# First block of a two-block transformer: weight splits off GpSimd, rotated halves kept in place, scores as 32-row products of four heads, the first expert quad interleaved

## The chip, the cores and the metric

The kernel runs on one core of one Trainium2 chip. The metric is the device time of one execution in microseconds, as the median of the runs shown. The engines of the core are named as in the profile: PE (TensorE, matmuls), PEld (its weight loads), DVE (VectorE), ACT (ScalarE), POOL (GpSimd) and SP (SyncE, which issues most of the DMAs).

## The reference

A sequence of 256 tokens of width 1024 goes through two blocks in fp32. The change touches the first one:

```python
def hybrid_mixer(h, positions, w_in, ...):
    z, xbc, dt_raw, q, k, v, g_ssd, g_att = split_columns(h @ w_in)
    y_ssd = ssd_mixer(z, xbc, dt_raw, ...) @ w_ssd_out
    q = rope(q.reshape(b, L, ATT_HEADS, ATT_HEAD_DIM), positions)   # 16 heads of 64
    k = rope(k.reshape(b, L, ATT_HEADS, ATT_HEAD_DIM), positions)
    y_att = moba_attention(q, k, v).reshape(b, L, ATT_INNER) @ w_attn_out
    merged = jax.nn.sigmoid(g_ssd) * y_ssd + jax.nn.sigmoid(g_att) * y_att
    return merged @ w_out

def rope(x, positions):
    ...
    x1, x2 = x[..., :half], x[..., half:]
    return jnp.concatenate([x1 * cos - x2 * sin, x2 * cos + x1 * sin], axis=-1)
```

With 256 tokens and attention blocks of 256 there is one block, so `moba_attention` is causal attention. The mixer's result is added to x. Then a hierarchical mixture of experts follows (4 groups of 8 experts of width 256, the best group and in it the two best experts of each token), and a gated addition of a second embedding. The second block (long convolutions and a latent attention) is untouched by the change.

## The kernel before

**Weights.** The products of the first block run in a reduced fp32 format of PE (`fp32r`). A weight tile is loaded as it is (`w`, 128x1024, through a ring of four buffers); ACT copies it into that format (`wsh`), and the rest, `w - wsh`, becomes `wsl`. The class `Split` makes the three, and each 1024-deep product is summed from three: wsh times the high part of x, wsh times its low part, wsl times its high part. `wsh` and `wsl` have three buffers each, so the split of a tile waits until PE is through with an older one. The subtraction runs on DVE (line 155) or, where the table `APL` lists the load, on POOL (line 230); the table lists 19 of them. Two further ones at the very start are shared between DVE and POOL in both kernels.

**Order.** The program is written as Python, and a scheduler puts each engine's instructions in an order by priority: as written, with shifts for tagged parts (`hp("k0")` and the table `HPD`). On the chip each engine works through its own list in order; an instruction that waits holds up all behind it.

**The mixer.** First come v, xbc and dt (`pv`, `pxbc`, `vdt`, `dtr`), with the short convolution on DVE (`cv`, then `xf`) and a chain of small operations for dt (`e`, `den`, `sv`, `sq`, `pl`, 128x32 each). PE transposes `xf` to tokens (`pxt`) and DVE scales it (`xdt`). Then four groups follow, of four heads each. A group projects q and k (`pq`, `pk`, 48 matmuls each), rotates them (`rope`), computes a part of the SSD mixer (`pr`, `L`, `py`) and attention (`attn_group`): scores (`psc`), row maxima by a custom DVE operation (lines 677 and 679), their scaling (`mx`), exponentials on ACT, a division by the row sums (`pt`), transposes of the probabilities (`ptp`, line 699) and the product with v (`po`). The q of the next group is projected between the scores: `advance(steps, n)` issues n matmuls of it (in group 3 it is a gate, `pg`).

**Rotation and scores before.** The projection leaves the first halves of four heads on one tile and the second halves on another, 32 rows a head. `rope` makes products with cos and sin on DVE (`rA`, `rB`), subtracts for the first half on DVE, over both slots at once, and adds for the second half on POOL (line 724), four times 32x256, each of which writes to other rows than it reads, so that a head stands in 64 rows. The scores of a head are then one product of 64 rows for the first 128 queries and one for the last 128 (over 256 keys): eight a group, and six matmuls of the next q behind each.

**Experts.** Tokens are sorted into slots of eight quads (four experts each, 32 slots an expert). A quad gathers its tokens by a product with a one-hot matrix (`pxe`, copied and scaled into `xe` by ACT and DVE), multiplies by the gate and up weights (`pgu`; `gate_up` takes two of eight 128-row slices), then by the down weights (`pyd`), and adds back (`acc`). The weights come as 192 loads of 512 KB (`we`), issued on SP into slots, 24 a quad; 49 slots are filled ahead of the first quad. Each load waits until the matmuls that read its slot are done. The first quad gathers everything before its first `gate_up`.

## Time and profile before

| | us |
|---|---|
| median of the 3 runs shown | 805.27 |
| lowest and highest of them | 805.26, 809.57 |
| the profiled execution | 805.95 |
| its span in the trace | 804.2 |
| PE busy | 766.6 (95% of the span) |
| DVE busy | 478.6 (60%) |
| ACT busy | 345.0 (43%) |
| POOL busy | 135.1 (17%) |

Busy times are sums over the whole span; the stages have different limits, so the rows further below are taken by stage. The mixer ends at about 226 us, its output projections and the routing at about 329, the experts at about 540, and the rest is the second block.

### The profile page before, as it was taken

Reading aid. Unit: us, or ns where it says so; the run is one execution under the profiler, and the core shown is the slowest. Engines: PE = TensorE matmul, PEld = TensorE weight load, DVE = VectorE, ACT = ScalarE, POOL = GpSimd, SP = SyncE. Lnnn points to the kernel's source line nnn. Section 1 sums busy time; section 2 is a strip of 40 time slices with the busy share of each in tenths; the row PEclk is TensorE's granted clock in tenths of the full one; section 3 lists DMA queues with packets and bytes.
Section 4 is the critical chain, followed back from the end, with each engine's and each line's share of the span. In section 5 each row is a group of like instructions: output and inputs, shape, how many; then the busy total and the mean of one; then the engine's idle time right before and its main releaser. Section 6 shows DMA issues by size and latency. Waiting matters only on the chain. (4 is left out here: it accounts for less than half of the span.)

```text
span 804.2 us, 14032 instructions
## 1 busy us (share of the span) xinstructions
PE 766.6 (95%) x5515; PEld 608.9 (76%) x5515; DVE 478.6 (60%) x932; ACT 345.0 (43%) x659; POOL 135.1 (17%) x147
## 2 busy tenths in 40 slices
PE   8996989998999999999999999889999999999997
PEld 7996878786799999645534343249999878888997
DVE  6788767887752555522243433047877887866662
ACT  6573453646544443012113112047757426555541
POOL 3713631333033310000000000100112540000000
PEclk9998999999999999999999999999999999999999
DMA  7653554243279989599999999976445231632561
GB/s 258 219 185 101 184 182 156 84 153 131 80 249 329 346 327 394 227 410 413 382 384 419 417 417 409 393 317 218 124 138 195 95 131 53 191 98 82 175 189 53
DMA packets 53204, 187.19 MB, mean 233 GB/s; under 512 B 5886, under 2 KB 8190, under 8 KB 53071
## 3 DMA queue, kind: packets, MB, share of 16 engines
q1 hardware_dynamic: 52736, 184.93, 63.3%
q0 software_dynamic: 400, 1.34, 0.4%
q8 instruction: 44, 0.72, 0.3%
q14 instruction: 24, 0.20, 0.1%
HBM read 185.20 MB, written 1.05 MB: 232 GB/s over the span
## 5 line engine op out<-in xcount | busy, mean ns | idle before, releaser
L152 ACT ACTIVATE wsh<-w 128x1024 fp32r<-128x1024 f32 (+2 forms) x148 | 153.8, 1043 | 144.4 <-issue 23.4
L155 DVE TENSOR_TENSOR wsl<-w,wsh 128x1024 fp32r<-128x1024 f32 (+3 forms) x127 | 155.8, 1231 | 67.8 <-ACT wsh L152 67.5
L143 PE MATMUL pgu<-we,xe 128*32 128x512 f32 x512 | 79.9, 599 | 4.3 <-DMA we<-in_w_e 4.0
L143 PEld LDWEIGHTS pgu<-we,xe 128*32 128x32 f32 x512 | 17.6, 109 | 55.2 <-issue 30.4
L230 POOL TENSOR_TENSOR wsl<-w,wsh 128x1024 fp32r<-128x1024 f32 x19 | 45.9, 2418 | 71.6 <-ACT wsh L152 71.4
L143 PE MATMUL pg<-h,wsh 128*128 128x256 f32 x256 | 47.1, 284 | 0.0
L143 PEld LDWEIGHTS pg<-h,wsh 128*128 128x128 f32 x256 | 39.6, 189 | 0.4 <-issue 0.2
L143 PE MATMUL pwo<-wsh,mh 128*128 128x256 f32 x128 | 36.1, 283 | 0.5 <-DVE x_t L164 0.5
L143 PE MATMUL pg<-h,wsl 128*128 128x256 f32 x128 | 36.2, 283 | 0.0
L143 PEld LDWEIGHTS pxe<-oh,x_t 128*128 128x128 f32 x256 | 30.0, 191 | 8.1 <-issue 4.2
L143 PE MATMUL pwo<-wsl,mh 128*128 128x256 f32 x128 | 36.1, 283 | 0.0
L143 PE MATMUL pwo<-wsh,ml 128*128 128x256 f32 x128 | 35.9, 282 | 0.0
L143 PE MATMUL pxe<-oh,x_t 128*128 128x128 f32 x256 | 33.0, 283 | 0.9 <-DVE xe L159 0.9
L143 PE MATMUL pyd<-we,hT 128*32 128x512 f32 x256 | 31.7, 597 | 1.2 <-ACT hT L152 0.7
L164 DVE SCALAR_TENSOR_TENSOR thm<-thm,pgu 128x256 f32<-128x256 f32 x8 | 3.4, 422 | 48.1 <-ACT thm L152 48.1
L143 PE MATMUL pq<-h,wsh 128*128 128x256 f32 x128 | 29.1, 319 | 0.0
L143 PE MATMUL pxbc<-h,wsh 128*128 128x256 f32 x160 | 28.5, 281 | 0.0
L1191 POOL DMA_DIRECT2D pT__5280<-in_p x1 | 0.8, 792 | 150.7 <-DMA we<-in_w_e 150.7
L155 DVE TENSOR_TENSOR Yl<-pyd,Yh 128x512 fp32r<-128x512 f32 x14 | 9.7, 692 | 27.4 <-ACT Yh L152 27.4
L143 PE MATMUL pz<-h,wsh 128*128 128x256 f32 x128 | 25.6, 291 | 0.0
L143 PEld LDWEIGHTS pq<-h,wsh 128*128 128x128 f32 x128 | 21.3, 204 | 5.5 <-issue 4.0
L143 PEld LDWEIGHTS pwo<-wsh,mh 128*128 128x128 f32 x128 | 24.3, 190 | 0.7 <-DVE x_t L164 0.7
(473 smaller groups left out, 2125.0 us busy)
## 6 DMA issues: line engine op xcount, KB each, us to landing
we<-in_w_e SPq DMA_DIRECT2D x192, 512.0 KB, 10.0
w<-in_w_a SPq DMA_DIRECT2D x74, 512.0 KB, 4.2
w<-in_w_c SPq DMA_DIRECT2D x66, 512.0 KB, 3.8
w<-in_w_vdt SPq DMA_DIRECT2D x8, 520.0 KB, 4.0
x_t<-in_x SPq DMA_DIRECT2D x2, 512.0 KB, 4.6
raw_ple<-in_w_ple POOLq DMA_DIRECT2D x2, 512.0 KB, 8.7
w<-in_w_c SPq DMA_DIRECT2D x2, 384.0 KB, 3.2
out<-x_t SPq DMA_DIRECT2D x3, 256.0 KB, 2.4
```

Of the source, the lines that this page charges most:

```text
L143: return PE.matmul(out=out, lhsT=lhsT, rhs=rhs, start=start, stop=stop, **k)
L152: return S.activation(out=out, in_=in_, func=func, **k)
L155: return V.tensor_tensor(out=out, in0=in0, in1=in1, op=op)
L164: return V.scalar_tensor_tensor(out=out, in0=in0, scalar=s, in1=in1, op0=op0, op1=op1)
L230: G.tensor_tensor(out=lo, in0=raw, in1=hi.bitcast(F32), op=OP.subtract)
L1191: G.dma_start(pT, a["p"])
```

## The change

The table `APL` is empty, so every subtraction of a weight split runs on DVE. `rope` leaves the first half of four heads on slot 0 and the second half on slot 1, head e on rows 32e to 32e+31, with one DVE operation of 128x256 each and none on POOL. The scores of a head are a sum of two 32-row products (first halves, second halves); the four heads of a group stand side by side on the array's rows, eight products in a row for each half of the queries, and 24 matmuls of the next q follow. In the product with v both heads' first product comes before both heads' second. The first quad gathers half of its slices, starts `gate_up`, and gathers the rest in between. The order of the second block is as before.

```diff
--- before.py
+++ after.py
@@ -43,7 +43,7 @@
 VH = (0,)
 XS = 256
 W0 = 50
-APL = {0: (0,), 10: (0,), 16: (0,), 18: (0,), 2: (0,), 22: (1,), 23: (1,), 24: (1,), 26: (1,), 27: (0,), 28: (0,), 31: (0,), 33: (0,), 4: (1,), 5: (0, 1), 6: (0,), 8: (0, 1)}
+APL = {}
...
@@ -128,7 +128,6 @@
 def tile_two_blocks(ctx: ExitStack, tc: tile.TileContext, a: dict, tap=None, upto="all"):
     nc = tc.nc
     V, S, G, PE, SP = nc.vector, nc.scalar, nc.gpsimd, nc.tensor, nc.sync
-    SH = G
     tap = tap or (lambda name, ap: None)
 
     def pool(stack, name, bufs=1, **k):
@@ -663,11 +662,12 @@
         def attn_group(i, q, k, steps):
             pss = [psum("sc", [P, 3, P], f"psc{e}") for e in range(4)]
             for t in range(NT):
-                for e in range(4):
-                    r = slice(64 * (e // 2), 64 * (e // 2) + 64)
-                    o = pss[e][:, 0, :] if t == 0 else pss[e][:, 1:3, :]
-                    mm(o, q[r, e % 2, t * P : (t + 1) * P], k[r, e % 2, 0 : (t + 1) * P], True, True)
-                    advance(steps, AST[i])
+                for half in range(2):
+                    for e in range(4):
+                        r = slice(32 * e, 32 * e + 32)
+                        o = pss[e][:, 0, :] if t == 0 else pss[e][:, 1:3, :]
+                        mm(o, q[r, half, t * P : (t + 1) * P], k[r, half, 0 : (t + 1) * P], half == 0, half == 1)
+                advance(steps, 4 * AST[i])
             advance(steps, 99)
             pt = mid.tile([P, 4, 3, P], F32, tag="t6", name="pt", bufs=2)
             mx = small.tile([P, 4, 2], F32, tag="mx", name="mx", bufs=2)
@@ -704,11 +704,14 @@
                         else:
                             V.tensor_copy(pT, ptp)
                     pts.append(pT)
-                for e in range(2):
-                    hs = slice(64 * (2 * hq + e), 64 * (2 * hq + e) + 64)
-                    o = po[64 * e : 64 * e + 64, :]
-                    mm(o, vdt[:, 0, i, hs], pts[e][:, 0:2, :], True, False)
-                    mm(o[:, P:], vdt[:, 1, i, hs], pts[e][:, 2, :], False, True)
+                for b in range(2):
+                    for e in range(2):
+                        hs = slice(64 * (2 * hq + e), 64 * (2 * hq + e) + 64)
+                        o = po[64 * e : 64 * e + 64, :]
+                        if b == 0:
+                            mm(o, vdt[:, 0, i, hs], pts[e][:, 0:2, :], True, False, skip_group_check=True)
+                        else:
+                            mm(o[:, P:], vdt[:, 1, i, hs], pts[e][:, 2, :], False, True, skip_group_check=True)
                 r = 2 * i + hq
                 with hp(f"as{i}"):
                     to_split(po, at[0][:, r, :], at[1][:, r, :])
@@ -718,10 +721,8 @@
             tt(A, p, cos_t.rearrange("p (o l) -> p o l", o=1).broadcast_to([P, 2, T]), OP.mult)
             tt(Bm, p, sin_t.rearrange("p (o l) -> p o l", o=1).broadcast_to([P, 2, T]), OP.mult)
             r = rope_p.tile([P, 2, T], F32, tag="uq", name=tag + "r", bufs=2)
-            tt(r, A[:, 0:1, :].broadcast_to([P, 2, T]), Bm[:, 1:2, :].broadcast_to([P, 2, T]), OP.subtract)
-            for e in range(4):
-                i, o = 32 * e, 32 * (e ^ 1)
-                SH.tensor_tensor(out=r[o : o + 32, e % 2, :], in0=A[i : i + 32, 1, :], in1=Bm[i : i + 32, 0, :], op=OP.add)
+            tt(r[:, 0, :], A[:, 0, :], Bm[:, 1, :], OP.subtract)
+            tt(r[:, 1, :], A[:, 1, :], Bm[:, 0, :], OP.add)
             return r
 
         def prefetch(n, after=None):
@@ -980,8 +981,8 @@
             if filler is not None:
                 next(filler, None)
 
-        def gather(q):
-            for k in range(0, KD, 2):
+        def gather(q, ks=range(0, KD, 2)):
+            for k in ks:
                 p = psum("tr", [P, 2, P], "pxe")
                 for i in range(2):
                     for t in range(NT):
@@ -1052,23 +1053,31 @@
             last = q == NQ - 1
             if q == 0:
                 make_oh(0)
-                gather(0)
-                combine_weights()
             wg, wd = quad_weights(q)
             if not last:
                 quad_weights(q + 1)
                 make_oh(q + 1)
             pg = psum("mm", [P, 512], "pgu")
-            gate_up(q, (0, 1), pg, wg)
-            while waiting:
-                waiting.pop()()
             if q == 0:
+                gather(0, (0, 2))
+                gate_up(0, (0, 1), pg, wg)
+                gather(0, (4,))
+                gate_up(0, (2, 3), pg, wg)
+                gather(0, (6,))
+                gate_up(0, (4, 5), pg, wg)
+                combine_weights()
                 slot_weights(0)
-            slot_rows(q)
-            fill()
-            for k in range(2, KD, 2):
-                gate_up(q, (k, k + 1), pg, wg)
+                slot_rows(0)
+                gate_up(0, (6, 7), pg, wg)
+            else:
+                gate_up(q, (0, 1), pg, wg)
+                while waiting:
+                    waiting.pop()()
+                slot_rows(q)
                 fill()
+                for k in range(2, KD, 2):
+                    gate_up(q, (k, k + 1), pg, wg)
+                    fill()
             hr, cs = scales.pop(q)
             th = mo.tile([P, T], F32, tag="Yh", name="thm")
             act(th, pg[:, 0:T], AF.Tanh, scale=hr)
```

PE around the scores of group 0 (`psc` with a number for each head, `pq` the q of group 1); before, the first two heads' products:

```order
L143 MATMUL psc_1205<-kr,qr 128x128
L143 MATMUL pq<-h_184,wsh 128x256 x2
L143 MATMUL pq<-h_184,wsl 128x256
L143 MATMUL pq<-h_184,wsh 128x256 x2
L143 MATMUL pq<-h_184,wsl 128x256
L143 MATMUL psc_1206<-kr,qr 128x128
L143 MATMUL pq<-h_185,wsh 128x256 x2
```

and after, from the first product to the beginning of the matmuls of q:

```order
L142 MATMUL psc_1199<-kr,qr 128x128
L142 MATMUL psc_1200<-kr,qr 128x128
L142 MATMUL psc_1201<-kr,qr 128x128
L142 MATMUL psc_1202<-kr,qr 128x128
L142 MATMUL psc_1199<-kr,qr 128x128
L142 MATMUL psc_1200<-kr,qr 128x128
L142 MATMUL psc_1201<-kr,qr 128x128
L142 MATMUL psc_1202<-kr,qr 128x128
L142 MATMUL pq<-h_184,wsh 128x256 x2
L142 MATMUL pq<-h_184,wsl 128x256
```

The products of the four heads come together now, twice four of them for each half of the queries, and the six matmuls that stood behind each became 24 behind eight. The second eight (`psc` 128x256) stand behind these 24.

DVE in the stretch that makes dt and the last two `xf`; before (the weight splits of this stretch stand in POOL's list, five in a row):

```order
L164 SCALAR_TENSOR_TENSOR pl<-pl,sq_916 128x32 x7
L164 SCALAR_TENSOR_TENSOR cv<-u,cw,cv 128x256
L164 SCALAR_TENSOR_TENSOR pl<-pl,sv 128x32
L164 SCALAR_TENSOR_TENSOR cv<-u,cw,cv 128x256
L164 SCALAR_TENSOR_TENSOR dt<-pl,dt 128x32
L164 SCALAR_TENSOR_TENSOR cv<-u,cw,cv 128x256
L164 SCALAR_TENSOR_TENSOR da<-dt,ae 128x32
L752 COPY da_1054<-da 128x2x16 x2
L164 SCALAR_TENSOR_TENSOR xf<-th,cv 128x256
L164 SCALAR_TENSOR_TENSOR cv<-u,cw,cv 128x256 x3
L155 TENSOR_TENSOR xdt<-pxt,dt 128x512 x2
L164 SCALAR_TENSOR_TENSOR xf<-th,cv 128x256
```

and after:

```order
L163 SCALAR_TENSOR_TENSOR pl<-pl,sq_916 128x32 x2
L154 TENSOR_TENSOR wsl<-w,wsh 128x1024
L163 SCALAR_TENSOR_TENSOR pl<-pl,sq_916 128x32
L163 SCALAR_TENSOR_TENSOR cv<-u,cw,cv 128x256
L163 SCALAR_TENSOR_TENSOR pl<-pl,sq_916 128x32
L163 SCALAR_TENSOR_TENSOR cv<-u,cw,cv 128x256
L163 SCALAR_TENSOR_TENSOR pl<-pl,sq_916 128x32
L163 SCALAR_TENSOR_TENSOR cv<-u,cw,cv 128x256
L163 SCALAR_TENSOR_TENSOR pl<-pl,sq_916 128x32 x2
L154 TENSOR_TENSOR wsl<-w,wsh 128x1024
L163 SCALAR_TENSOR_TENSOR pl<-pl,sv 128x32
L163 SCALAR_TENSOR_TENSOR xf<-th,cv 128x256
```

Two splits moved in ahead of the first `xf` of the piece (one more stands some rows above), and two rows that made copies of `da` moved behind it. In each group of heads DVE's list changes in a second place: before, `rA` and `rB` of the next q stood between the last row maximum and `mx`; now `mx` stands directly behind the maxima, and in groups 0 and 1 a weight split stands directly ahead of the first of them.

PE in the first quad; before:

```order
L143 MATMUL pxe<-oh,x_t 128x128 x16
L143 MATMUL pgu<-we,xe 32x512 x8
L143 MATMUL pcs<-comb,oh 128x5 x2
L871 MATMUL pqt<-cst,oh 128x128 x2
L143 MATMUL pgu<-we,xe 32x512 x24
```

and after:

```order
L142 MATMUL pxe<-oh,x_t 128x128 x8
L142 MATMUL pgu<-we,xe 32x512 x8
L142 MATMUL pxe<-oh,x_t 128x128 x4
L142 MATMUL pgu<-we,xe 32x512 x8
L142 MATMUL pxe<-oh,x_t 128x128 x4
L142 MATMUL pgu<-we,xe 32x512 x8
L142 MATMUL pcs<-comb,oh 128x5 x2
L872 MATMUL pqt<-cst,oh 128x128 x2
L142 MATMUL pgu<-we,xe 32x512 x8
```

Half of the gathers are now ahead of the first eight `pgu`, and the weights of the slots (`pcs`, `pqt`) stand behind 24 of the 32.

## Rows read from the trace of the kernel before

**Rows 1.** Stretches of the span: busy us and instructions, granted clock, DMA share, GB/s.

```profile
60.00:83.00 23.00, 16.77 (x117) 16.11 (x116) 20.05 (x37) 8.52 (x15) 6.78 (x3) 0.85 0.39 129
83.00:112.00 29.00, 27.75 (x203) 24.39 (x201) 18.59 (x35) 10.95 (x24) 17.48 (x15) 1.00 0.63 222
...
226.00:300.00 74.00, 74.00 (x632) 74.00 (x631) 34.40 (x35) 33.43 (x37) 24.52 (x20) 1.00 0.90 325
...
328.50:338.50 10.00, 8.87 (x81) 6.23 (x85) 6.54 (x43) 1.67 (x5) 0.00 (x0) 1.00 0.17 52
338.50:500.00 161.50, 154.30 (x1002) 67.91 (x998) 56.02 (x142) 33.38 (x68) 1.87 (x3) 1.00 1.02 407
```

**Rows 2.** What PE waited for from 0 to 345 us: total, times, longest.

```profile
PE ptp L699 <- DVE pt L159: 6.6, 8, 2.2
PE pxt L569 <- DVE xf L164: 6.2, 2, 4.3
```

**Rows 3.** PE from 60 to 84 us: start, duration, instruction, idle before and its releaser.

```profile
69.83 0.78 PE L143 MATMUL pq<-h,wsh 128*128 128x256 f32 x2
...
73.45 0.44 PE L569 MATMUL pxt<-cst,xf 128*128 128x128 f32 x2 [1.98 <-DVE xf L164]
```

**Rows 4.** DVE from 54 to 80 us, same columns.

```profile
58.30 0.17 DVE L159 TENSOR_SCALAR dt<-dtr 128x32 f32<-128x32 f32 x1
...
59.73 2.38 DVE L159 TENSOR_SCALAR pl<-sq 128x32 f32<-128x32 f32 x1
...
67.73 0.43 DVE L164 SCALAR_TENSOR_TENSOR xf<-th,cv 128x256 f32<-128x256 f32 x1
68.22 3.65 DVE L164 SCALAR_TENSOR_TENSOR cv<-u,cw,cv 128x256 f32<-128x256 f32 x3
```

**Rows 5.** POOL from 54 to 112 us, same columns.

```profile
59.67 4.73 POOL L230 TENSOR_TENSOR wsl<-w,wsh 128x1024 fp32r<-128x1024 f32 x2 [1.34 <-ACT wsh L152]
69.22 2.37 POOL L230 TENSOR_TENSOR wsl<-w,wsh 128x1024 fp32r<-128x1024 f32 x1 [4.81 <-ACT wsh L152]
```

**Rows 6.** PE around the scores of group 0, 92 to 116 us.

```profile
93.66 0.49 PE L143 MATMUL psc<-kr,qr 64*128 64x128 f32 x2
...
94.97 0.49 PE L143 MATMUL psc<-kr,qr 64*128 64x128 f32 x2
...
104.93 0.40 PE L143 MATMUL pk<-h,wsh 128*128 128x256 f32 x2
...
110.23 0.40 PE L143 MATMUL pk<-h,wsh 128*128 128x256 f32 x2
```

**Rows 7.** PE at the scores of group 3, 200 to 208 us.

```profile
203.27 2.00 PE L143 MATMUL psc<-kr,qr 64*128 64x128 f32 x16
205.21 0.38 PE L143 MATMUL pao<-ath,wsh 128*128 128x256 f32 x1
```

**Rows 8.** DVE behind the scores of group 0, 103 to 114 us.

```profile
105.19 0.69 DVE L155 TENSOR_TENSOR rA<-pq,sincos 128x512 f32<-128x512 f32 x1 [0.32 <-issue]
...
106.40 2.23 DVE L159 TENSOR_SCALAR mx<-mx 128x8 f32<-128x8 f32 x1
```

**Rows 9.** PE at the end of that chain.

```profile
112.98 0.30 PE L699 MATMUL ptp<-cst,pt 128*128 128x128 f32 x1 [2.23 <-DVE pt L159]
```

**Rows 10.** DVE by shape, 0 to 345 us: count, busy, mean ns, idle before and releaser.

```profile
L155 DVE TENSOR_TENSOR wsl<-w,wsh 128x1024 fp32r<-128x1024 f32 x55 | 68.6, 1249 | 42.7 <-ACT wsh L152 42.5
...
L679 DVE CUSTOM_DVE_ANT_0 pt<-psc,msk 128x256 f32<-128x256 f32 x16 | 6.7, 417 | 0.0
...
L677 DVE CUSTOM_DVE_ANT_0 pt<-psc,msk 128x128 f32<-128x128 f32 x16 | 4.6, 287 | 9.8 <-PE psc L143 9.8
```

**Rows 11.** PE in the first quad, 329 to 345 us.

```profile
330.99 3.95 PE L143 MATMUL pxe<-oh,x_t 128*128 128x128 f32 x32
334.88 1.92 PE L143 MATMUL pgu<-we,xe 128*32 128x512 f32 x16
...
337.54 5.36 PE L143 MATMUL pgu<-we,xe 128*32 128x512 f32 x48
```

## The prediction

> **What bounds the kernel now.** I read the stretches of the span first [rows 1]. PE is the engine that sets the end almost everywhere: from 226 to 300 us it is busy for 74.00 of 74.00 us, and where it is not full one finds the places that a change can win. There are three kinds. From 60 to 83 us it works for 16.77 of 23.00, and the granted clock there is 0.85. In the groups of heads it is nearly full (27.75 of 29.00), so that there only work that is taken off PE itself counts, and short waits. From 328.5 to 338.5 the DMA share is 0.17 and from 338.5 to 500 it is 1.02: the experts' weights come without a break from there, PE waits for some of them, and so the time at which this stream starts again sets when the experts end. The view of waits up to 345 us [rows 2] names what PE waits for: 6.6 us in eight waits for the probabilities (`ptp`), and 6.2 us in two for `xf`. A microsecond saved before 226 us moves all that follows, because the order behind it is the same and the prefetch of expert weights goes on from slots that PE frees.
>
> **Splits on DVE, and the stretch at 60 us.** On POOL a split takes 2.37 us [rows 5] and on DVE 1.249 [rows 10], so the 19 of the table bring DVE 23.7 us. Eight of the 19 lie between 226 and 300 us, where PE is full and DVE works for 34.40 of 74 us [rows 1]: nothing is won or lost there; without that room each would cost up to 1.25. In the front the trace shows what the POOL splits cost DVE. A `dt` operation of 128x32 takes 0.17; the like one that starts beside the split at 59.67 takes 2.38, about until that split would be through [rows 4, 5]. Three `cv` take 3.65 beside the split of 2.37 at 69.22. So a DVE instruction can stand still for a whole POOL split, and moving the split costs DVE its 1.2 us but gives back up to 2.2. For the first `xf` (67.73): of 59.73 to 67.73 the like chain without locks is 8 operations of `pl` at 0.18, three `cv` at some 0.48 (a third of 3.65 less 2.2), and three small ones, 3.5 to 4; two splits add 2.4, so about 6 instead of 8. Another lock of 2 us, some rows above, gives its place to one more split. I put this `xf` 2.5 to 3.4 us earlier, which takes the wait of 4.25 (6.2 less the second one's 1.98 [rows 2, 3]) to about 1.3. The second `xf` loses its lock (2.2) but gets two `xdt` ahead; I leave it 1.3 of its 1.98. That is 6.2 to 2.6, or 3.6 us won.
>
> With the waits goes the clock. Behind the first wait two matmuls of q take 0.78 us [rows 3], where the like two of k take 0.40 later [rows 6]: PE runs at 1.2 GHz instead of 2.4 there. A mean of 0.85 over 23 us is 3.4 us of full clock not granted; about a quarter falls into the waits themselves. I price the rest at 2.5. Whether waits of 1.3 us still lose the clock no row tells at this place, but the wait of 2.23 at 112.98 [rows 9], with dense work ahead, lies at the end of a stretch that shows 1.00 [rows 1]. I count 1.9 of the 2.5 as won. Together −5.5; ends −2 (the splits wait in line for ACT and the clock falls again) and −8.7 (all of it).
>
> **Scores.** From the first product of group 0 to the first `pk` it is 11.27 us [rows 6]. In it PE runs eight products and 48 matmuls of q. A matmul of this kind takes 0.118 (45 from 104.93 to 110.23), so 48 take 5.65 and the eight products 5.62. One product and its way in and out of PE's 64-row form cost 0.60: the distance 1.31 of the first two, less six matmuls at 0.118. In group 3 the same eight stand together, and take 1.94 to the next matmul (203.27 to 205.21) [rows 7]; 0.24 each (there are two records a product) instead of 0.70, which I read as two things: one way in and out for all, and two at a time side by side, as they hold different halves of the rows. So four rounds and one way in and out are 1.94. The changed group also has four rounds, two of four heads each for either half of the queries, if four run side by side, but two ways in and out: 1.94 and some 0.3 (half of 0.60), 2.2 in all. That gives 3.4 us for each of groups 0 to 2, −10.2, and nothing in group 3. Ends: only two side by side, eight rounds, 3.6 to 3.9 a group, a loss of 1.7 in group 3, −3.5; and rounds slightly cheaper than in group 3, −10.6. I take −10.2, by the row of the same operands. On four rows of the array no row here can speak. The Trainium skill ("TensorE: Matmul & The Clock Gate", section "Measured speedup vs the span model") gives 3.07 times, not four, for four products of 32 rows and 512 columns; by it each round would be 1.3 times as long, about half a microsecond a group, and the time below would be 789.4 instead of 787.4.
>
> The rotation gets shorter by the POOL part, but PE has `pz` to do in between, and no wait for `psc` is among the waits [rows 2]: nothing. Without that cover it would be a gain too. The two heads' products with v already run next to each other; their new order is worth −0.3 to 0; I take 0.
>
> **Probabilities.** In group 0, `ptp` waits 2.23 us [rows 9]. Ahead of the exponentials `mx` took 2.23 us beside a POOL split, behind `rA` and `rB` of the next q [rows 8]; now it stands ahead of these (1.21 from 105.19 to 106.40) and has no lock (2.0 of the 2.23): 3.2 earlier. Against that, seven of the eight maxima start only behind the second eight products, 2.6 us (four at 0.417, three at 0.287 [rows 10]) instead of the last pair's 0.7, which is 1.8, and a split of 1.25 ahead of them may be late (0.4 counted). PE's cover gets smaller too: 49 matmuls instead of 54, 0.6. So 2.23 becomes 1.8. In group 1 the lock was not there and the later maxima are, so a short wait becomes about as long; in group 2, with the whole of k ahead, they nearly vanish. Over all I take 6.6 to 4.3, −2.3; ends −6.6 and +1.
>
> **First quad.** The loads wait until the first `pgu` have read their slots. These started at 334.88, behind all gathers (330.99 on, 3.89 us); now they start behind half of them, at 332.95 [rows 11]: −1.9. DVE and ACT have had `xe` of the first slices ready by then; if they are late, −0.5 is left. The three more changes between the two forms of product lie on PE, which is ahead of the DMAs from the fifth quad on. What PE saves otherwise (`pcs` later) is hidden.
>
> **New waits.** DVE was busy for 20.05 of 23 us and 18.59 of 29 [rows 1], and 11 splits come to it there. What it evacuates in the SSD part (`L` for `py`) may be late now. No row shows it; the nearest are the waits for `ptp`, 0.8 on average and 2.2 at most [rows 2]. I put 2.0 for all groups, ends 0 and 5.
>
> **The sum.** The profiled execution took 805.95 us. 805.95 − 5.5 − 10.2 − 2.3 − 1.9 + 2.0 = 788.05. The median of the runs is 805.27, 0.68 below, so I forecast 787.4.
>
> **Rivals.** *The evacuation takes it back.* Maxima, exponentials and scaling of a group start together, behind the second eight products, with a split ahead; what PE saves at the scores comes back as waits at `ptp` and `py`, since DVE and ACT get no less work by it. Then the 10.2 are gone: 797.6. For it speaks the wait of 2.23, which is there already; against it, that the chain in group 0 loses 3.2 us of its own. The Trainium skill ("TensorEngine Tiling (Array Packing)", section "PSUM Bottleneck") says that tiling makes TensorE faster but not the evacuation of PSUM; that would be this case.
>
> *All waits go.* Both `xf` in time with full clock (−8.7), `ptp` (−6.6) and no new ones: 805.95 − 8.7 − 10.6 − 6.6 − 1.9 = 778.15, as a median 777.5. DVE's load speaks against it.
>
> *The stream of weights sets the end alone.* Then the front's savings are waited for at the experts and only the restart counts: 805.95 − 1.9, as a median 803.4. Against it: a DMA share of 0.63 at the groups, and of 0.90 before 300, with PE full [rows 1].
>
> *Slower.* The 32-row products do not run side by side, and each pays for itself what a 64-row one pays alone: 16 at 0.70 (5.62 by eight) are 11.2 us a group, 5.6 more in three groups and 9.3 more in group 3: 805.95 − 5.5 − 2.3 − 1.9 + 2.0 + 26.1 = 824.35, a median of 823.7. From 6.6 us a group on, 0.41 a product, the time would lie above that of before; group 3's rows speak against it, where neighbours share a form and overlap.
>
> **How the numbers follow.** Forecast with its bounds 0.70, all waits go 0.10, evacuation 0.12, stream 0.05, slower 0.03. About 1% (8 us) is what a measurement of this kernel can tell from no change. Faster is the first two and some of the third, 0.83; the same 0.14; slower 0.03. The range of 777 to 799 takes in the two ends at 777.5 and 797.6, and leaves out the last two.
>
> **What would show it.** In the changed profile: no row of 2 us for a small DVE operation ahead of 226 us; the waits for `xf` below 3 us together and a clock near 1.00 from 60 to 83; four `psc` at a time with one start, and 7.8 us from the first of them to the first `pk`; waits for `ptp` of about 4 us; the first `pgu` 2 us behind the first gather instead of 3.9, and the DMA share back at 1 as much earlier. Wrong would be: `psc` one by one, waits for `py` or `ptp` of over 10 us, or the experts' end moving less than the front.

## The result, and the profile after

The median went from 805.26 us (4 runs, 804.89 to 809.57) to 786.69 (4 runs, 786.36 to 788.82); the ratio is 0.9766 with a 95% interval of 0.9734 to 0.9799, so the changed kernel is 2.0 to 2.7% faster. Forecast were 787.4, in a range of 777 to 799. The profiled execution took 786.77 us and its span is 785.0, against 805.95 and 804.2. All rows below are read against these two.

The page: engine totals, and the granted clock in 40 slices.

```profile
PE 750.4 (96%) x5579; PEld 601.5 (77%) x5579; DVE 474.1 (60%) x959; ACT 345.5 (44%) x659; POOL 58.8 (7%) x96
...
PEclk9999999999999999999999999999999999999999
```

DVE and ACT are as busy as before (474.1 and 345.5 us in all), POOL has 58.8 us instead of 135.1, and PE works 16 us less. Where the 19.2 us of the span went, stretch by stretch (each from the first instruction named to the next one, on PE):

| stretch | before | after | difference |
|---|---|---|---|
| start to the first transpose of `xf` | 63.14 | 63.78 | +0.6 |
| on to the sums of dt (`pac`) | 16.95 | 8.07 | −8.9 |
| `pac` to the first score of group 0 | 13.57 | 13.57 | 0.0 |
| group 0, to the first score of group 1 | 33.15 | 29.13 | −4.0 |
| group 1, to the first score of group 2 | 30.53 | 29.08 | −1.5 |
| groups 2 and 3, to `pso` | 99.24 | 96.89 | −2.3 |
| `pso` to the first gather (`pxe`) | 74.41 | 74.56 | +0.1 |
| first gather to the last `pyd` | 202.95 | 199.56 | −3.4 |
| the rest | 270.3 | 270.4 | +0.1 |

**The stretch at 60 us.** The waits of PE up to 330 us (total, times, longest; rows of waits that both kernels have are left out), the stretch itself, and PE and DVE in it:

```profile
PE ptp L699 <- DVE pt L158: 6.2, 4, 2.0
...
PE pss L142 <- DVE sqs L642: 0.7, 1, 0.7
PE pao L142 <- DVE m L163: 0.7, 1, 0.7
PE pxt L568 <- DVE xf L163: 0.5, 1, 0.5
```

```profile
60.00:83.00 23.00, 22.54 (x191) 21.84 (x190) 22.33 (x51) 11.81 (x19) 0.00 (x0) 1.00 0.66 227
85.40:240.50 155.10, 147.55 (x1213) 129.94 (x1213) 108.94 (x236) 79.82 (x182) 5.28 (x10) 1.00 0.50 172
```

```profile
63.78 1.69 PE L568 MATMUL pxt<-cst,xf 128*128 128x128 f32 x14
...
67.22 0.44 PE L568 MATMUL pxt<-cst,xf 128*128 128x128 f32 x2 [0.46 <-DVE xf L163]
```

```profile
59.00 0.18 DVE L158 TENSOR_SCALAR pl<-sq 128x32 f32<-128x32 f32 x1
...
59.55 1.23 DVE L154 TENSOR_TENSOR wsl<-w,wsh 128x1024 fp32r<-128x1024 f32 x1
...
62.56 1.22 DVE L154 TENSOR_TENSOR wsl<-w,wsh 128x1024 fp32r<-128x1024 f32 x1
...
63.80 0.42 DVE L163 SCALAR_TENSOR_TENSOR xf<-th,cv 128x256 f32<-128x256 f32 x1
```

The two waits for `xf`, 6.2 us in [rows 2], have become one of 0.46, and the stretch shows 22.54 us of work in 23 and a clock of 1.00, where [rows 1] had 16.77 and 0.85. The `pl` operation that took 2.38 beside a POOL split [rows 4] takes 0.18. The splits stand in line on DVE, two in these rows, and `xf` is still there at 63.80 instead of 67.73.

**Scores.** PE in group 0 and group 3:

```profile
85.42 0.73 PE L142 MATMUL psc<-kr,qr 32*128 32x128 f32 x16
...
89.11 1.15 PE L142 MATMUL psc<-kr,qr 32*128 32x256 f32 x16
...
93.13 0.41 PE L142 MATMUL pk<-h,wsh 128*128 128x256 f32 x2
```

```profile
183.06 2.70 PE L142 MATMUL psc<-kr,qr 32*128 32x128 f32 x32
185.69 0.51 PE L142 MATMUL pg<-h,wsh 128*128 128x256 f32 x2
```

From the first score to the first `pk` it is 7.71 us instead of 11.27 [rows 6], less 5.65 for the 48 matmuls of q 2.06 for the sixteen products; 2.2 had been forecast. Four products start within 20 ns of each other in the trace, so four do run side by side. In group 2 the same piece took 9.87 us instead of 12.60; the small products of the SSD norm (`pss`, `prs`) lie in it in both kernels, with a wait of 0.69 instead of 0.17, so that 3.2 us are won there without the waits. In group 3, though, the sixteen take 2.63 us to the next matmul, where the eight took 1.94 [rows 7]: there the fourth head's products start 1.1 us behind the other three's, and products of both widths mix.

**The chain behind the scores.** DVE and PE in group 0:

```profile
90.19 1.23 DVE L154 TENSOR_TENSOR wsl<-w,wsh 128x1024 fp32r<-128x1024 f32 x1 [1.86 <-ACT wsh L151]
91.33 0.28 DVE L677 CUSTOM_DVE_ANT_0 pt<-psc,msk 128x128 f32<-128x128 f32 x1
...
93.67 0.17 DVE L158 TENSOR_SCALAR mx<-mx 128x8 f32<-128x8 f32 x1
```

```profile
98.19 0.30 PE L699 MATMUL ptp<-cst,pt 128*128 128x128 f32 x1 [1.95 <-DVE pt L158]
```

The second eight products end at 90.25. The maxima, those of the first eight products too, start at 91.33, behind a split that itself waited for ACT; `mx` is done at 93.84, the transposes start at 98.19 and PE has waited 1.95 us, which is hardly less than the 2.23 of before [rows 9]. In group 1 the wait grew from 0.4 in all to 1.96. In group 2, where before had 3.2 us in five waits, there is one of 1.88. DVE, ACT and PE there:

```profile
152.49 0.28 DVE L677 CUSTOM_DVE_ANT_0 pt<-psc,msk 128x128 f32<-128x128 f32 x1
```

```profile
155.44 1.04 ACT L151 ACTIVATE wsh<-w 128x1024 fp32r<-128x1024 f32 x1
...
158.64 1.04 ACT L151 ACTIVATE wsh<-w 128x1024 fp32r<-128x1024 f32 x1
```

```profile
161.43 0.33 PE L699 MATMUL ptp<-cst,pt 128*128 128x128 f32 x1 [1.88 <-DVE pt L158]
```

The whole of k stands ahead of the transposes there (74 matmuls instead of 49 in group 0), but the chain takes 10.8 us from the end of the second eight products (150.59) to the first transpose, instead of 7.9: the maxima start 1.9 us late, behind a split and operations of the SSD norm, and two copies of weights (`wsh`) stand among the exponentials on ACT. All `ptp` waits together are 6.2 us, as against 6.6.

**First quad.** PE:

```profile
315.08 1.95 PE L142 MATMUL pxe<-oh,x_t 128*128 128x128 f32 x16
316.96 1.92 PE L142 MATMUL pgu<-we,xe 128*32 128x512 f32 x16
318.82 1.16 PE L142 MATMUL pxe<-oh,x_t 128*128 128x128 f32 x8
```

The first `pgu` stands 1.88 us behind the first gather (3.89 in [rows 11]).

### The profile page after: what moved, and what is told of

The parts are those of the page before. It is cut to its first block, busy times and chain, and to the rows that moved or that the text cites. A ratio compares the mean times of both kernels' runs of the same rounds, so it can differ in the third digit from the quotient of the medians.

```text
span 785.0 us, 14128 instructions
## 1 busy us (share of the span) xinstructions
PE 750.4 (96%) x5579; PEld 601.5 (77%) x5579; DVE 474.1 (60%) x959; ACT 345.5 (44%) x659; POOL 58.8 (7%) x96
## 5 line engine op out<-in xcount | busy, mean ns | idle before, releaser
L154 DVE TENSOR_TENSOR wsl<-w,wsh 128x1024 fp32r<-128x1024 f32 (+3 forms) x146 | 177.7, 1221 | 72.4 <-ACT wsh L151 71.8
L142 PE MATMUL pgu<-we,xe 128*32 128x512 f32 x512 | 75.3, 598 | 4.1 <-DMA we<-in_w_e 3.8
L142 PE MATMUL pv<-wsh,h 128*128 128x260 f32 x128 | 24.1, 285 | 0.8 <-ACT h L151 0.8
L142 PE MATMUL pk<-h,wsh 128*128 128x256 f32 x128 | 24.7, 288 | 0.0
L142 PEld LDWEIGHTS pxbc<-h,wsh 128*128 128x128 f32 x160 | 24.5, 189 | 0.0
L142 PEld LDWEIGHTS pg<-h,wsl 128*128 128x128 f32 x128 | 24.2, 189 | 0.2 <-issue 0.2
L142 PEld LDWEIGHTS pwo<-wsl,mh 128*128 128x128 f32 x128 | 24.3, 190 | 0.0
```

The source lines that it names most:

```text
L142: return PE.matmul(out=out, lhsT=lhsT, rhs=rhs, start=start, stop=stop, **k)
L154: return V.tensor_tensor(out=out, in0=in0, in1=in1, op=op)
```

## The experiments

Times are medians; "before" in a row is the kernel before on the same chip, whose median was 805.2 to 805.7 in all three sessions.

| kernel | us | ratio to before, 95% |
|---|---|---|
| splits on DVE alone | 798.28 | 0.9906 (0.9878 to 0.9934) |
| 64-row scores put together, alone | 816.51 | 1.0128 (1.0087 to 1.0169) |
| changed, 32-row scores taken apart | 804.38 | 0.9975 (0.9941 to 1.0010) |
| first quad alone | 802.87 | 0.9970 (0.9949 to 0.9992) |
| changed, splits back on POOL | 803.53 | 0.9966 (0.9948 to 0.9983) |
| 64-row scores together, splits on DVE | 797.90 | 0.9888 (0.9858 to 0.9918) |
| changed, 12 + 36 matmuls of q | 783.97 | 0.9735 (0.9716 to 0.9755) |
| changed, 0 + 48 matmuls of q | 792.85 | 0.9840 (0.9818 to 0.9862) |
| the same with 12 + 36, norm later | 780.20 | 0.9675 (0.9653 to 0.9697) |
| changed, once more | 790.00 | 0.9798 (0.9769 to 0.9826) |
| changed, products with v as before | 788.27 | 0.9786 (0.9754 to 0.9818) |
| changed, second rotated half on POOL | 791.96 | 0.9838 (0.9810 to 0.9866) |

### Splits on DVE alone

```diff
 # the kernel before
-APL = {0: (0,), 10: (0,), 16: (0,), ...
+APL = {}
```

> The kernel before with the table of POOL splits emptied, nothing else. Theory (POOL splits hold DVE up, and xf with it): from the first transpose of xf to the sums of dt (pac) it takes about 8.1 us instead of 16.95, the clock stays at 1.00 from 60 to 83 us, and the time is 795 to 798. Rival (the gain at 60 us hangs on the shorter rotation and the order of the rest): over 4 us of waits for xf stay and the time is 801 or more. Second rival (23.7 us more on DVE cost elsewhere what they win): 803 or more with new waits for L, pt or wsl.

From the first transpose of `xf` to `pac` it took 8.08 us, at full clock: the gain at 60 us is this edit, all of it. The time is 798.28, 0.3 above the upper end of the first theory. Its waits on PE:

```profile
PE pao L143 <- ACT tg L152: 4.6, 1, 4.6
PE ptp L699 <- DVE pt L159: 1.4, 3, 0.9
...
PE pxt L569 <- DVE xf L164: 0.5, 1, 0.5
```

The waits for `ptp` went down from 6.6 to 1.4 us here, with scores one by one; in the changed kernel they are 6.2. But a new wait of 4.6 us came up at `pao` in group 3, for a gate (`tg`) that stood in ACT's line behind eight exponentials, which waited for `mx`; behind it PE ran 6.8 us at half the clock. The span is 7.6 us shorter, not 8.9.

### First quad alone

```diff
 # the kernel before, with gather() and the head of quad() of the changed one
+                gather(0, (0, 2))
+                gate_up(0, (0, 1), pg, wg)
...
```

> The kernel before with the first quad of the changed one, nothing else. Theory (the experts' loads start again as soon as the first pgu have read their slots): the first pgu 1.9 us behind the first gather instead of 3.9, the last expert load 2.0 us earlier, and the time is 803.3. Rival (the 3.4 us that the changed kernel wins between the gathers and the last pyd are all from this edit): 801.9. Second rival (the stream is paced by later matmuls): within 0.5 us of before.

The first `pgu` came 1.88 us behind the first gather, and from there to the last `pyd` it took 199.49 us instead of 202.95: −3.5, which is what the changed kernel shows (−3.4). So all of it is from this edit, as the first rival has it; the time, 802.87, lies between the two forecasts and nearer to that of the theory. The issues of the expert loads (counted from the first gather) came 2.0 us earlier in both kernels at the first load behind the gather, 2.6 to 3.5 earlier at load 112 and 3.4 at the last one. The first number is the restart that was forecast; where the stream wins the rest was not found.

### Scores of 64 rows put together, alone

```diff
 # the kernel before
-                for e in range(4):
+                for e in (0, 2, 1, 3):
                     r = slice(64 * (e // 2), 64 * (e // 2) + 64)
                     ...
-                    advance(steps, AST[i])
+                advance(steps, 4 * AST[i])
```

> The kernel before with its 64-row score products put together, four in a row for each half of the queries (heads in the order 0, 2, 1, 3) and 24 matmuls of the next q behind; rotation, splits and first quad as before. Theory (what a score product costs is its way in and out of the form, so that grouping brings the gain and 32 rows bring none): from the first psc to pk in group 0 it takes 7.7 to 8.0 us instead of 11.27, and the time is 795 to 798. Rival (it takes four heads side by side): 9.5 or more, and 800 or more.

Slower by 11 us: neither of the two. From the first score to the next `pk` it took 8.00 us in group 1, as the theory of the way in and out says, but 10.43 in group 0, of which 2.0 are waits for `kr` from POOL. What costs is elsewhere. PE in group 2, and POOL ahead of it:

```profile
178.03 0.58 PE L143 MATMUL pz<-h,wsl 128*128 128x256 f32 x1 [5.68 <-POOL wsl L230]
```

```profile
171.50 4.06 POOL L724 TENSOR_TENSOR qr<-rA,rB 32x256 f32<-32x256 f32 x3 [7.36 <-DVE qr L155]
175.64 2.34 POOL L230 TENSOR_TENSOR wsl<-w,wsh 128x1024 fp32r<-128x1024 f32 x1
```

Products with z wait 5.68 us for a split on POOL, which stands in POOL's line behind additions of the rotation, and these wait for DVE. Over the stretch from 40 to 345 us PE stands still for 24.4 us (14.9 before), and the clock is at half for 30.7 us in it, where it was 6.8 before.

### The same with the splits on DVE

```diff
 # the kernel above
-APL = {0: (0,), 10: (0,), 16: (0,), ...
+APL = {}
```

> The kernel before with the table of POOL splits emptied and its 64-row products put together (heads in the order 0, 2, 1, 3); the second halves of the rotation still on POOL, first quad as before. Theory (grouping brings the gain, 32 rows none; POOL's splits were what spoiled it): from the first psc to pk under 8.5 us in each of groups 0 to 2 apart from waits for the rotation, no wait for wsl, and the time is 787 to 792. Rival (the 32-row form and the short rotation are needed): 795 or more.

No wait for a split is left in the groups but one of 1.0 us, and 18.6 us come back against the kernel above; but the time, 797.90, is that of the splits alone (798.28), above the theory's 787 to 792 and where the rival put it (795 or more). In group 1, with 0.86 us of waiting for `kr` taken off, the piece from the first score to `pk` is 8.2 us: put together, 64-row products are nearly as cheap as the 32-row ones (7.7). So of the rival's two conditions this piece speaks against the 32-row form. (In group 0 it is 11.3 without these waits, 6.8 of them at half the clock.) The gain is lost again at waits of PE:

```profile
PE ptp L699 <- DVE pt L159: 6.0, 7, 2.0
PE psc L143 <- POOL kr L724: 3.8, 4, 1.2
```

3.8 us are for the rotation on POOL, which the changed kernel hasn't; the waits for `ptp` rise from 1.4 with the splits alone to 6.0, which is what they are in the changed kernel (6.2); and 13.7 us at half the clock follow these waits.

### Scores of 32 rows taken apart

```diff
 # the changed kernel
-                for half in range(2):
-                    for e in range(4):
+                for e in range(4):
+                    for half in range(2):
                         ...
-                advance(steps, 4 * AST[i])
+                    advance(steps, AST[i])
```

> The changed kernel with its 32-row products taken apart again: both halves of one head, then six matmuls of the next q, head by head. Theory (way in and out): from the first psc to pk in group 0 it takes 11 us or more instead of 7.7, and the time is 795 to 799. Rival (32-row products are cheap by themselves): 9 us or less, and 791 or less.

PE in group 0:

```profile
85.47 0.71 PE L142 MATMUL psc<-kr,qr 32*128 32x128 f32 x4
...
87.02 0.71 PE L142 MATMUL psc<-kr,qr 32*128 32x128 f32 x4
...
99.38 0.39 PE L142 MATMUL pk<-h,wsh 128*128 128x256 f32 x2
```

From the first score to `pk` it is 13.91 us, 8.26 for the products, over three times the 2.06 of the changed kernel and more than the eight 64-row products took one by one (5.62). So the theory of the way in and out holds in kind (what that way consists of, no row shows), and its price was too low; the time, 804.38, is above the range of both. The waits for `ptp` are 2.7 us here instead of 6.2. Four heads side by side are thus not a saving by themselves: of 6.2 us between apart and together in a group, all lies in putting the products together. Of the 17.7 us between the two kernels' medians some 3 come only at the experts, which is taken up with the kernel with the later norm.

### The changed kernel with its splits back on POOL

```diff
 # the changed kernel
-APL = {}
+APL = {0: (0,), 10: (0,), 16: (0,), ...
```

> The changed kernel with the 19 splits given back to POOL. Theory 1 (the edits add up; POOL splits cost only the stretch at 60 us): 8.9 us more, 795 to 797, and nothing new in the groups. Theory 2 (a group that got shorter runs into POOL's slow splits, as the 64-row grouping alone showed with a wait of 5.7 us for a POOL split): over 799, with waits of PE for wsl from POOL behind 93 us.

803.53: theory 2 in the amount, but not by its mechanism. No wait for a split shows. The stretch at 60 us is back at 18.02 us, and group 0 takes 36.78 us instead of 29.13. DVE, POOL and PE there, and the stretch as a whole:

```profile
107.58 4.02 DVE L158 TENSOR_SCALAR pt<-pt,sm 128x128 f32<-128x128 f32 x8
```

```profile
108.33 2.46 POOL L229 TENSOR_TENSOR wsl<-w,wsh 128x1024 fp32r<-128x1024 f32 x1 [12.31 <-ACT wsh L151]
```

```profile
108.01 0.30 PE L699 MATMUL ptp<-cst,pt 128*128 128x128 f32 x1 [2.00 <-DVE pt L158]
...
111.03 1.09 PE L699 MATMUL ptp<-cst,pt 128*128 128x128 f32 x4 [1.91 <-DVE pt L158]
```

```profile
95.20:132.00 36.80, 32.89 (x233) 26.70 (x232) 22.30 (x50) 15.20 (x40) 3.28 (x2) 0.81 0.37 128
```

The scaling of the probabilities takes 4.02 us for eight operations, since a POOL split starts at 108.33 beside them. PE gets a second wait of 1.91 shortly behind the one of 2.00, and in the second the clock falls to half for 13.7 us, which costs some 6.8 us. So group 0 is 7.65 us longer, which began with one split of 2.46 us on another engine; the changed kernel, run once more below, shows that the first wait alone can be followed by 3.4 us at half the clock, so that up to 1.7 of these 7.65 us come without the split. Alone, the POOL table cost 7.6 us of span; inside the changed kernel it costs 17.5 against the execution shown above and 12.4 against the second one below, and 13.5 to 16.8 by the medians.

### 12, or none, of the matmuls of q between the two halves of the scores

```diff
 # the changed kernel
-AST = (6, 6, 6, 6)
+AST = (3, 3, 3, 6)     # the other kernel: (0, 0, 0, 6)
```

> The changed kernel with 12 instead of 24 matmuls of the next q behind the first eight score products of groups 0 to 2, and the other 36 behind the second eight. Theory (ptp waits because the chain of maxima, exponentials and scaling starts behind the second eight and has too little beside it): the waits for ptp in groups 0 to 2 fall from 5.8 us to under 1.5, and the time is 781 to 783. Rival (DVE and ACT set the pace of a group, so that the wait shows up elsewhere): 785 or more.

> The changed kernel with all sixteen score products of groups 0 to 2 in a row and the 48 matmuls of the next q behind them. Theory as for 12: waits for ptp under 2.5 us in groups 0 to 2, and one way in and out less a group (0.3 each): 781 to 783. Rival as for 12: 785 or more.

With 12 the forecast holds but for one microsecond: 783.97. The waits for `ptp`, and DVE in group 0:

```profile
PE ptp L699 <- DVE pt L158: 0.9, 2, 0.5
```

```profile
88.62 0.29 DVE L677 CUSTOM_DVE_ANT_0 pt<-psc,msk 128x128 f32<-128x128 f32 x1 [0.53 <-PE psc L142]
...
90.97 0.17 DVE L158 TENSOR_SCALAR mx<-mx 128x8 f32<-128x8 f32 x1
```

A split stands behind the maxima now, the first of them starts with the end of the second eight products (88.61), and the `ptp` waits of the first two groups are gone (0.9 us in all, in groups 2 and 3). PE's work there is the same: 7.69 us from the first score to `pk`. Two things changed at once. From the end of the second eight products to the first transpose it is 7.14 us instead of 7.94, or 0.8 less, as nothing holds the maxima up; and 59 matmuls stand in between instead of 49, which is 1.2 us more of PE's work. Together they are the 1.95 us of the wait; no run has one of them without the other.

With none between, the products end even earlier (86.48), but a split and one more operation stand ahead of the maxima again (they start at 87.71) and PE has 49 matmuls beside the chain, as in the changed kernel. It waits 2.11 us in groups 0 and 1, and the clock falls each time for 3.4 us, and for 10.2 us behind a wait for the SSD norm: 792.85, above both medians of the changed kernel (786.69, and 790.00 below) and in the rival's range, not the theory's. So the theory's condition, enough work beside the chain, isn't met by this edit. DVE and ACT have the same work in all three kernels, and it depends on the order what of their time PE sees.

### The norm later, and the changed kernel once more

```diff
 # the kernel with 12 + 36, in ssd_norm()
             for t in range(NT):
-                mm(p[:, t : t + 1], ...)
+                with tc.high_priority(-200):
+                    mm(p[:, t : t + 1], ...)
...
+            with tc.high_priority(-200):
+                mm(rs, ones, ...)
```

> The changed kernel with 12 matmuls behind the first eight score products, as before, and the two small products of the SSD norm (pss, prs) put later in PE's order. Theory (what is left in group 2 of that kernel is PE standing at pss and prs, 1.8 us, and 3.4 us at half the clock behind it): 780 to 782. Rival (the later norm comes back at the products that need its result): 784 or more.

> The changed kernel once more, word for word, beside the others on one chip: 786 to 788; the kernel with 12 matmuls behind the first eight products (783.97) is better than it by more than chance if its own time here lies above 785.5.

The first gives 780.20, 3.25% under the kernel before, and is the best of all. The changed kernel on the same chip took 790.00 this time, above the 786 to 788 that were expected, and its profiled execution 5.1 us of span more than that shown above. Its waits for `ptp`, and the stretch of the groups:

```profile
PE ptp L699 <- DVE pt L158: 6.1, 4, 2.0
```

```profile
85.00:245.80 160.80, 153.33 (x1214) 134.83 (x1214) 109.36 (x236) 79.88 (x182) 5.29 (x10) 0.96 0.49 167
```

The waits for `ptp` are the same to 0.1 us (6.1 against 6.2), and by the bound set ahead the kernel with 12 + 36 (783.97) is the better one; its slowest run (785.55) is below the fastest of the changed kernel in either session (786.36), though the first interval of the changed kernel's ratio (0.9734 to 0.9799) overlaps with its own. But the clock over the groups is 0.96 instead of 1.00: it fell to half four times for 3.4 us, each time behind one of the waits of 0.7 to 2 us. The same stretch of the best kernel has no wait over 0.6 us and no fall:

```profile
85.00:231.40 146.40, 145.77 (x1212) 128.79 (x1213) 109.08 (x236) 80.11 (x182) 3.47 (x10) 1.00 0.52 176
```

PE is busy for 145.77 of 146.40 us there. Its experts take longer in return (203.6 us from the first gather to the last `pyd`, instead of 199.6), and wait for weights at `pyd`, where the changed kernel has all its waits for them (3.8 us) at `pgu`:

```profile
PE pyd L142 <- DMA we<-in_w_e: 3.4, 3, 2.9
PE pgu L142 <- DMA we<-in_w_e: 2.0, 7, 0.6
```

Of 9.2 us that the front won against the execution shown above, 5.2 were left at the last `pyd`. That looks like the rival of the weight stream, but SP's list shows another cause. SP comes once to a branch of the program (L1228, over a path for tokens that find no slot) and issues no load there for some 8 us. SP's waits from 486 to 501 us and its loads in this kernel:

```profile
SPq L1228 <- SPq L1228: 6.8, 3, 5.2
```

```profile
488.37 1.59 SPq L381 DMA_DIRECT2D we<-in_w_e  x2
498.08 0.88 SPq L247 DMA_DIRECT2D w<-in_w_c  x2
499.06 0.84 SPq L381 DMA_DIRECT2D we<-in_w_e  x2
```

and the last loads of the changed kernel:

```profile
500.43 2.45 SPq L381 DMA_DIRECT2D we<-in_w_e  x3
```

In the changed kernel the branch is reached 161 us behind the first gather. Here it is reached after 185 us, ahead of the last two expert loads (and of two loads of the second block, `w`), so that the last one is issued 6.2 us later, counted from the first gather. The kernel with the 32-row products taken apart reaches it after 184 us, has the same wait (2.7 us at one `pyd`) and takes 202.8 us for its experts, although they begin 22 us later than here. So it is the place of the branch in SP's order, and not a front that has become short enough. What this kernel would take with the branch in its old place was not run.

### The two small parts

```diff
 # the changed kernel, (1) products with v again head by head
-                for b in range(2):
-                    for e in range(2):
...
+                for e in range(2):
+                    mm(o, vdt[:, 0, i, hs], pts[e][:, 0:2, :], True, False)
+                    mm(o[:, P:], vdt[:, 1, i, hs], pts[e][:, 2, :], False, True)
 # (2) rope()
-            tt(r[:, 1, :], A[:, 1, :], Bm[:, 0, :], OP.add)
+            G.tensor_tensor(out=r[:, 1, :], in0=A[:, 1, :], in1=Bm[:, 0, :], op=OP.add)
```

> The changed kernel with the order of the products with v as before. Theory (they ran side by side before): within 1 us of the changed kernel, 785.5 to 788. Rival (the new order matters): 789 or more.

> The changed kernel with the second half of the rotation on POOL, one addition of 128x256, where the kernel before had four of 32x256. Theory (what hurts is POOL beside DVE: a rotation that PE waits for, and DVE held up): psc waits for kr from POOL by 0.3 to 1 us a group and small DVE operations beside the addition take over 1 us; 787 to 791. Rival (one short addition is hidden behind pz): within 1 us of the changed kernel.

Beside the changed kernel of the same session (790.00) the first has 788.27, the second 791.96; the intervals overlap in both. The order of the products with v is worth nothing that shows. The second half on POOL as one addition (0.7 to 1.7 us) brings no wait for `kr`, and its group 0 is like the changed kernel's (30.50 us against 30.45), as the rival says; the time is 2 us above instead of within 1, and PE waits 2.5 us for DVE at `pss`, `prs` and `psc`, where the changed kernel waits 1.4 at `pss` and `pao`, so that some cost isn't excluded. The waits for `kr` of the kernels with 64-row products put together thus go with the four additions of 32x256, 3.2 to 5.8 us a rotation there, more than with the place of the work.

## Why the prediction was right

The sign, the size and the two main mechanisms were right; of its terms three were off by 1.5 to 3.4 us, and the errors partly cancel. That the sum came within 0.7 us of the median is luck; the same kernel took 790.00 in another session.

- **Splits and `xf`: −5.5 forecast, −8.9 measured, with its direction and cause shown** by the splits alone (8.08 us against 16.95). The term was sized too small: 1.3 us were left to each of the two waits and 0.6 to the clock, and the kernel has one wait of 0.46 and full clock. The lower end, −8.7, was about right.
- **Scores: −10.2 forecast; 3.6 us in groups 0 and 1, 3.2 in group 2 and +0.7 in group 3, −9.7.** The row of group 3, from which the size was taken, was a good measure, although the two forms differ. The step that held less well is the one on group 3 itself, where nothing was expected. That four run side by side, which no row of before could say, is now seen; the rounds cost no more than those of two 64-row products (0.11 us at 128 columns and 0.22 at 256). So the figure of 3.07 times from the Trainium skill ("TensorE: Matmul & The Clock Gate", section "Measured speedup vs the span model"), by which the time would have been 2 us longer, isn't borne out at these widths; no run has its 512 columns.
- **Probabilities: −2.3 forecast, −0.4 measured.** This step failed, and in group 2. The lock at `mx` went (2.23 to 0.17 us), and in group 0 the sum was right: 1.8 forecast, 1.95 measured, although the split ahead of the maxima held them up by 1.1 instead of 0.4; group 1 has 1.96, about as forecast. But in group 2 the wait was to vanish with the whole of k ahead, and it is 1.88, since the SSD norm and the weight copies lengthen the chain there. By the runs, the emptied table alone takes the waits from 6.6 to 1.4, and putting the products together brings them back (6.0 with 64 rows, 6.2 here). With 12 matmuls between the halves they fall to 0.9.
- **First quad: −1.9 forecast, −3.4 measured**, by the quad alone −3.5. The restart was sized rightly (2.0); the other 1.4 come later in the stream and aren't explained.
- **New waits: +2.0 forecast.** `py` doesn't wait. `pss` and `pao` wait 1.2 us more, and some 1.3 us of the groups that no wait shows lie among the matmuls of k, z and the small products between them, whose order is another; they were not taken apart.

What was wrong beneath a right sum is that its terms were added. The same table of splits is worth 7.6 us alone and 12.4 to 17.5 in the changed kernel, by the execution that one compares with; putting 64-row products together makes the old kernel slower, and without the emptied table the rest of the change is worth 1.7 us of span. The rows above point at the reason: shorter groups leave less PE work beside the same chains on DVE, ACT and POOL, and what PE waits for, it pays for about twice where the clock falls.

Of the rivals, the one of the evacuation was half there: 5.8 us of `ptp` waits stayed, and cost more where the clock fell behind them. The rule of the Trainium skill ("TensorEngine Tiling (Array Packing)", section "PSUM Bottleneck") points at it. With 12 + 36 matmuls the waits go with the same work on DVE and ACT, so that the order decided here whether PE sees their time.

## What to carry to other kernels

Count what a small product costs on its way into and out of a form of the array before counting its columns: here 0.6 to 0.8 us for a 64-row product between full-width matmuls, and 0.13 for a 32-row one among its like. When PE gets faster between two fixed chains, look next at which instruction stands ahead of the first link of the chain on each in-order queue, and give PE's filler work to the side of the chain that is exposed. The queue that issues the loads is one of these: with a branch ahead of its last two expert loads the best kernel's experts took 203.6 us instead of 199.6. Measure edits that share engines together as well as alone; a second engine that holds up the first is cheap while there is slack and dear when there is none.

## What the runs showed of the hardware

- **A wait of 0.7 to 2 us can be followed by 3.4 us at half the clock, which costs 1.7 us more.** In two executions of one kernel with equal waits (6.1 and 6.2 us at `ptp`) the clock stayed at 1.00 in one and fell to half four times for 3.4 us in the other; the spans are 785.0 and 790.1. With two waits of 2 us one behind the other it was half for 13.7 us. The kernel without such waits spread over 778.3 to 780.7, the changed one over 786.4 to 793.0.
- **POOL holds DVE up far beyond small operations.** Eight scalings of 128x128 and 128x256 took 4.02 us beside one POOL split, and 1.93 without one in the kernel with 12 + 36; the chain behind them cost PE a second wait. The Trainium skill ("SBUF — State Buffer", section "Who interferes with whom") says of DVE operations that use the pair of ports which the two engines share that whoever issues first has it for the whole instruction and the other blocks, and the rows agree: 2.38 for an operation of 0.18 in [rows 4], against a split of 2.37.
- **Four 32-row products start within 20 ns and take 0.11 us a round at 128 columns and 0.22 at 256** (the distance from one start to the next behind the first round; the trace has two records, so two rounds, for each product), as two of 64 rows do; standing alone, the two halves of one head cost 0.8 to 1.3 us.
